# Whole fp32 operands in two products of each second projection's last piece, and a subtraction moved from GpSimd to VectorE

## The chip, the cores and the metric

The kernel runs on one core of a Trainium2 chip. Its engines are TensorE (PE in the profile; its weight loads are listed as PEld), VectorE (DVE), ScalarE (ACT), GpSimd (POOL) and SyncE (SP), which issues most DMAs. Each engine works through its own line of instructions in order and waits on semaphores of the others. The metric is the time of one execution on the device in microseconds; lower is better.

## The reference

A decoder trunk of two layers over 1024 positions with 1024 features, all in float32. Each layer is a token mixer and a gated feed-forward block (FFN), each behind an RMS norm with a scale and a shift that depend on the conditioning vector c.

```python
for layer in range(DEPTH):
    sh1, sc1, g1, sh2, sc2, g2 = jnp.split(c_act @ mod_w[layer] + mod_b[layer], 6, axis=-1)
    h = modulate(rmsnorm(x, norm_mix_g[layer]), sh1, sc1)
    y = dsa_mixer(h, ...) if layer == 0 else gmlp_mixer(h, ...)
    x = x + g1 * y
    h = modulate(rmsnorm(x, norm_ffn_g[layer]), sh2, sc2)
    x = x + g2 * ((silu(h @ w_gate) * (h @ w_up)) @ w_down)
return rmsnorm(x, final_g)

def gmlp_mixer(h, w_in, ln_g, ln_b, w_s, b_s, w_out):
    z = gelu(h @ w_in)
    u, v = z[..., :2048], layernorm(z[..., 2048:], ln_g, ln_b)
    v = v.reshape(B, 8, 128, 8, 256)                       # chunks of 128 positions, 8 groups
    mixed = einsum('gts,bcsge->bctge', w_s * tril, v) + b_s.T[:, :, None]
    return (u * mixed.reshape(B, T, 2048)) @ w_out
```

Layer 0 has the attention mixer, layer 1 the gMLP mixer.

## The kernel before

Activations stand transposed: features on the 128 partitions, positions along the free dimension, in two halves `ch` of 512 positions. Products that have to be precise are made from a value's high part (its cast to fp32r, by ScalarE) and its low part (the value less the high part, by VectorE or GpSimd); `mm3` (L177 to L181) adds three fp32r matmuls, high x high, high x low and low x high, in a PSUM bank.

There are four second projections, all made by `out_win` (L1009): the attention's output (one piece, n = 4), the first FFN's (pieces of 4, 4 and 3), the gMLP's (4 and 4) and the last FFN's (4, 4 and 3). A piece covers 2n blocks of 128 of the contracted features. Inside a piece the 2x2 blocks of weights (`wraw`, pages A and B) and of activations (`graw`, pages 1 and 2) are multiplied in Winograd's way, in seven products j in the order 1, 2, 6, 7, 4, 5, 3. Each product has 4 x n matmul groups. Before a product, `mv_prep` and `w_prep` make its sums from the raw pages and split them into high and low parts: `gm` (activations, n tiles, one page each) and `wst` (weights, 4 tiles). The cast is at L1057, the subtraction at L1058. Where the table `whole(pi)` names a product, the raw or summed fp32 values go to TensorE as they are, by L1164 instead of `mm3`:

```python
def whole(pi):
    if len(pieces) == 1:
        return RAW_1
    return RAW_F if pi == 0 else RAW_L if pi == len(pieces) - 1 else ()
```

Before, this holds for product 2 of a first piece where there are several pieces. After each group, `residual` (L952, VectorE) adds the PSUM bank times a gate to the residual stream `x`; the next product of the same four banks waits for it.

In the last piece, the norm of the next block begins between products: after product 4 the first half of `x` is complete, and `moving(ch=0)` makes its squares (`sqp`, ScalarE and VectorE), their sum over features on TensorE (`st`), the root, and a broadcast (`rb`, TensorE); `LOCK` puts part of product 5 behind `st` and part behind `rb`. Then VectorE makes `xr`, ScalarE `hq`, and they are split into `mv` for the next layer. Products 5 and 3 complete the second half, and `moving(ch=1)` follows.

The gMLP mixer loops over 8 groups g. A group makes seven products (3, 5, 4, 2, 1, 6, 7), each of four `mm3`, sums them on VectorE in pages `gu` and `uv`, and multiplies the four results with the mixed gate values `y` (`gate_fin`, L1537). The sum after product 7 is L1558; the first sums after products 3 and 2 are L1507. The gate values come from `mix_v`, one group ahead, twice for each group:

```python
ACT.copy(vh_, zg)
VL_ENG.tensor_sub(vl_, zg, f(vh_))
```

These are `vnh` (L1457) and `vnl` (L1458) of 128x1024; the mixing matmuls L1525 and L1526 read them. `VL_ENG` is GpSimd.

The order of each engine's line is written by a planner that simulates the program with estimated durations; `issue_after` adds single constraints. Tiles come from pools: 37 pages of 128x1024 fp32 (`pg`), 8 `wst` slots (`wsp`), 4 + 4 PSUM banks.

Of the kernel before, what the change touches and what calls it, by code (L numbers as in the profile page):

```python
# [102 lines left out]
PF_F = {3: 12, 2: 12, 7: 12, 6: 8, 5: 2}  # L103
PF_G = {4: 4, 2: 4, 7: 4, 1: 4, 3: 2, 6: 12}
VN_DVE = 1
RAW_F, RAW_1, RAW_L = (2,), (), ()
FF0 = (0,) * 6 + (4,) * 9 + (3,) * 4 + (0,) * 3
FF1 = (0,) * 8 + (1,) * 8 + (0,) * 6

# [4 lines left out]
def trunk(ctx, tc, xT, c, modT, vec, kgb, w_idx, w_q, w_a, wuk, wuv, wo, wg, wu, wd,  # L114
          bwu, bwv, bwo, bws, bbs, outT):
    nc = tc.nc
    PE, DVE, ACT, POOL, SP = nc.tensor, nc.vector, nc.scalar, nc.gpsimd, nc.sync
# [27 lines left out]
    def f(ap):  # L145
        return ap.bitcast(F32)
# [45 lines left out]
    SUM_ENG = {1: POOL, 2: POOL, 5: DVE, 6: POOL, 7: POOL}  # L192
    LO_ENG = {1: DVE, 2: DVE, 3: DVE, 4: POOL, 5: DVE, 6: DVE, 7: POOL}
    UA_ENG = POOL
    VL_ENG = POOL
    ident = cst.tile([P, P], F32, name="ident")
    make_identity(nc, ident)
    identr = cst.tile([P, P], F32R, name="identr")
# [1141 lines left out]
    def gmlp(x, B, pieces):  # L1340
# [104 lines left out]
        def mix_v(g, i):  # L1445
# [11 lines left out]
            ACT.copy(vh_, zg)  # L1457
            VL_ENG.tensor_sub(vl_, zg, f(vh_))  # L1458
            return vh_, vl_
# [222 lines left out]
```

## Time and profile before

| | |
|---|---|
| runs of the kernel before | 2596.45, 2601.79, 2601.98 us; median 2601.79 |
| the profiled execution | 2602.36 us, span 2600.7 us |
| mean granted clock of TensorE | 0.959 |
| busy, VectorE / ScalarE / GpSimd | 2133.6 / 1208.5 / 1344.0 us |

The span runs from the first to the last instruction of the program; the 1.7 us beside it are start and end. Times in rows are microseconds from the start of the span. In the rows, "out<-in" are the program's names, and what follows "idle before" is the time that the engine stood still just before the instruction, with what ended it.

### The profile page before, as it was taken

What the parts mean: (1) busy time and instruction counts of PE and PEld (TensorE: products, weight loads), DVE (VectorE), ACT (ScalarE), POOL (GpSimd) and SP (SyncE); (2) the same over time, 40 slices, a digit from 0 to 9 for tenths busy, and PEclk for the clock granted to TensorE, in tenths of its full rate; (3) what the DMA queues carried; (4) which work ended last, traced back from release to release, by engine and by line L of the source; (5) the groups of instructions that cost most, each with busy time, mean ns of one, the idle gap of its engine ahead of it and who ended that gap; (6) DMA issues with size and microseconds to landing.
All of it is one profiled execution on the core that took longest, in us unless ns stands there. A gap on an engine that the chain in (4) does not pass through costs nothing. (4 is left out here: it accounts for less than half of the span.)

```text
span 2600.7 us, 31048 instructions
## 1 busy us (share of the span) xinstructions
PE 2397.1 (92%) x10254; PEld 1877.9 (72%) x10254; DVE 2133.6 (82%) x3433; ACT 1208.5 (46%) x2223; POOL 1344.0 (52%) x962
## 2 busy tenths in 40 slices
PE   6979889988899999989988999988999999999996
PEld 4544577876688888768766877767767888886785
DVE  6497988898988888799878688899889666568986
ACT  5377775655533333343464454424464333333334
POOL 2021143465755556665556455566467444455663
PEclk7999899999999999999998999999999999999998
DMA  6002265645135544632123244363132223254021
GB/s 255 33 9 74 107 212 177 231 134 163 60 133 186 193 164 154 251 130 97 37 78 122 81 142 131 108 259 130 50 113 98 105 98 111 76 213 162 14 98 65
DMA packets 133919, 328.58 MB, mean 126 GB/s; under 512 B 14080, under 2 KB 30720, under 8 KB 133760
## 3 DMA queue, kind: packets, MB, share of 16 engines
q1 hardware_dynamic: 130432, 318.22, 34.7%
q0 software_dynamic: 3328, 8.39, 1.1%
q8 instruction: 81, 1.33, 0.2%
q14 instruction: 78, 0.64, 0.1%
HBM read 253.16 MB, written 73.40 MB: 126 GB/s over the span
## 5 line engine op out<-in xcount | busy, mean ns | idle before, releaser
L1239 PE MATMUL p<-mv,wst 128*128 128x512 f32 x1232 | 484.8, 394 | 9.2 <-DVE mv L967 9.2
L1240 PE MATMUL p<-mv,wst 128*128 128x512 f32 x1232 | 484.3, 393 | 7.2 <-DVE wst L1218 7.2
L1238 PE MATMUL p<-mv,wst 128*128 128x512 f32 x1232 | 483.1, 394 | 2.4 <-ACT wst L1217 0.9
L1216 POOL TENSOR_TENSOR wsum<-wgu 128x512 f32<-128x512 f32 x208 | 300.4, 1447 | 303.2 <-DVE wst L1218 198.4
L179 PE MATMUL d_ps<-gm,wst 128*128 128x512 f32 x904 | 366.2, 406 | 50.5 <-DVE x L952 44.6
L181 PE MATMUL d_ps<-gm,wst 128*128 128x512 f32 x904 | 359.0, 397 | 2.0 <-DVE wst L1058 2.0
L180 PE MATMUL d_ps<-gm,wst 128*128 128x512 f32 x904 | 359.3, 397 | 0.2 <-DVE gm L1058 0.2
L1239 PEld LDWEIGHTS p<-mv,wst 128*128 128x128 f32 x1232 | 233.7, 190 | 63.1 <-DVE mv L967 13.8
L1240 PEld LDWEIGHTS p<-mv,wst 128*128 128x128 f32 x1232 | 234.0, 190 | 57.8 <-DVE wst L1218 9.4
L1238 PEld LDWEIGHTS p<-mv,wst 128*128 128x128 f32 x1232 | 233.9, 190 | 54.8 <-issue 2.5
L1217 ACT CAST wst<-wsum 128x512 fp32r<-128x512 f32 x260 | 161.3, 621 | 216.9 <-POOL wsum L1216 97.1
L179 PEld LDWEIGHTS d_ps<-gm,wst 128*128 128x128 f32 x904 | 174.1, 193 | 98.9 <-ACT wst L1057 32.6
L1218 DVE TENSOR_TENSOR wst<-wsum,wst 128x512 fp32r<-128x512 f32 x208 | 200.6, 966 | 44.4 <-ACT wst L1217 43.4
L952 DVE SCALAR_TENSOR_TENSOR x<-d_ps,modv,x 128x512 f32<-128x512 f32 x252 | 185.0, 740 | 30.7 <-PE d_ps L181 30.7
L181 PEld LDWEIGHTS d_ps<-gm,wst 128*128 128x128 f32 x904 | 174.1, 193 | 40.7 <-DVE wst L1058 3.2
L180 PEld LDWEIGHTS d_ps<-gm,wst 128*128 128x128 f32 x904 | 174.6, 193 | 38.9 <-issue 1.7
L1058 POOL TENSOR_TENSOR gm<-graw,gm 128x512 fp32r<-128x512 f32 x102 | 158.8, 1566 | 81.9 <-ACT gm L1057 67.4
L1057 ACT CAST wst<-wraw 128x512 fp32r<-128x512 f32 (+1 forms) x204 | 117.3, 593 | 160.1 <-PE d_ps L181 137.2
L1057 ACT CAST gm<-graw 128x512 fp32r<-128x512 f32 x192 | 113.1, 618 | 102.2 <-DVE wst L1058 34.2
L1058 DVE TENSOR_TENSOR wst<-wraw,wst 128x512 fp32r<-128x512 f32 (+1 forms) x153 | 133.8, 878 | 13.2 <-ACT wst L1057 13.2
L1058 POOL TENSOR_TENSOR wst<-wraw,wst 128x512 fp32r<-128x512 f32 (+1 forms) x51 | 72.9, 1430 | 126.7 <-ACT wst L1057 126.7
L1217 ACT CAST wst<-wgu 128x512 fp32r<-128x512 f32 x104 | 64.3, 619 | 144.0 <-PE p L1240 70.8
(380 smaller groups left out, 5576.9 us busy)
## 6 DMA issues: line engine op xcount, KB each, us to landing
md<-modT SPq DMA_DIRECT2D x96, 512.0 KB, 5.3
wgu<-wg SPq DMA_DIRECT2D x56, 512.0 KB, 3.5
wgu<-wu SPq DMA_DIRECT2D x56, 512.0 KB, 4.4
g_d<-uv SPq DMA_DIRECT2D x88, 256.0 KB, 2.0
graw<-g_d SPq DMA_DIRECT2D x44, 512.0 KB, 7.6
wraw<-wd SPq DMA_DIRECT2D x64, 256.0 KB, 6.4
x_d<-x SPq DMA_DIRECT2D x48, 256.0 KB, 2.1
x<-x_d SPq DMA_DIRECT2D x24, 512.0 KB, 7.1
```

Source lines behind the costliest of these rows:

```text
L179: PE.matmul(ps, sh, mh, start=first, stop=False, skip_group_check=run)
L180: PE.matmul(ps, sh, ml, start=False, stop=False, skip_group_check=run)
L181: PE.matmul(ps, sl, mh, start=False, stop=last, skip_group_check=run)
L952: DVE.scalar_tensor_tensor(xk[:, cs], ps, gate, (xk[:, cs] if src is None else src), op0=ALU.mult, op1=ALU.add)
L1057: ACT.copy(t[:, 0, :n], s)
L1058: e.tensor_sub(t[:, 1, :n], s, f(t[:, 0, :n]))
L1216: SUM_ENG[j].tensor_tensor(s, o[0], o[1], op=o[2])
L1217: ACT.copy(t[:, 0], s)
L1218: LO_ENG[j].tensor_sub(t[:, 1], s, f(t[:, 0]))
L1238: PE.matmul(ps, sh, mh, start=k == 0, stop=False)
L1239: PE.matmul(ps, sh, ml, start=False, stop=False)
L1240: PE.matmul(ps, sl, mh, start=False, stop=k == 3)
```

## The change

Products 5 and 3 of the last piece of each second projection (the only piece of the attention's output) take their operands whole in fp32. `VL_ENG` becomes VectorE.

```diff
-RAW_F, RAW_1, RAW_L = (2,), (), ()
+RAW_F, RAW_1, RAW_L = (2,), (5, 3), (5, 3)
@@
-    VL_ENG = POOL
+    VL_ENG = DVE
```

## Rows read from the trace of the kernel before

**Rows 1.** The page, part 1: busy time, share of the span, instructions.

```profile
PE 2397.1 (92%) x10254; PEld 1877.9 (72%) x10254; DVE 2133.6 (82%) x3433; ACT 1208.5 (46%) x2223; POOL 1344.0 (52%) x962
```

**Rows 2.** Stretches: length, busy by engine (instructions), granted clock, DMA share, GB/s.

```profile
577.00:625.00 48.00, 40.41 (x161) 31.23 (x160) 42.71 (x73) 22.22 (x39) 20.78 (x14) 0.93 0.40 134
...
2537.00:2566.00 29.00, 22.58 (x88) 18.00 (x89) 23.25 (x33) 13.29 (x25) 7.67 (x6) 0.88 0.00 1
```

**Rows 3.** TensorE's waits, 575 to 645 us: us in total, times, longest.

```profile
PE d_ps L179 <- DVE x L952: 5.5, 4, 2.0
PE st L287 <- DVE sqp L284: 2.1, 1, 2.1
```

**Rows 4.** TensorE's waits, 1270 to 1340 us.

```profile
PE d_ps L179 <- ACT gm L1057: 4.6, 1, 4.6
PE z_ps L179 <- DVE xr L972: 2.5, 1, 2.5
...
PE d_ps L179 <- DVE x L952: 0.9, 1, 0.9
```

**Rows 5.** TensorE's waits, 1845 to 1912 us.

```profile
PE d_ps L179 <- DVE x L952: 4.0, 3, 1.7
```

**Rows 6.** TensorE's waits, 2535 us to the end.

```profile
PE d_ps L179 <- DVE x L952: 6.6, 2, 5.6
```

**Rows 7.** Timeline of VectorE from 2538 us: start, length, line, tiles, count.

```profile
2538.46 1.67 DVE L1058 TENSOR_TENSOR gm<-graw,gm 128x512 fp32r<-128x512 f32 x1
2540.06 1.62 DVE L1058 TENSOR_TENSOR wst<-wraw,wst 128x384 fp32r<-128x384 f32 x1
2541.60 0.74 DVE L952 SCALAR_TENSOR_TENSOR x<-d_ps,modv,x 128x512 f32<-128x512 f32 x1
```

**Rows 8.** TensorE's waits in the group loop, 1519 to 1714 us.

```profile
PE p L179 <- DVE uv L1558: 9.3, 4, 2.4
PE p L179 <- DVE uv L1507: 2.4, 2, 2.0
```

**Rows 9.** Timeline of VectorE in the group loop, from 1605 us.

```profile
1605.57 5.41 DVE L1537 TENSOR_TENSOR gu<-gu,y 128x512 f32<-128x512 f32 x2
1610.90 0.68 DVE L1558 TENSOR_TENSOR uv<-uv,p 128x512 f32<-128x512 f32 x1
```

**Rows 10.** Instructions of L1458: shortest/median/longest ns, first and last start.

```profile
L1458 POOLq EVENT_SEMAPHORE  x22: 17/43/4869, 1520.2 to 1687.3; - x22
L1458 POOL TENSOR_TENSOR vnl<-zg,vnh x16: 2390/2638/2946, 1521.4 to 1691.8; 128x1024 fp32r<-128x1024 f32 x16
```

**Rows 11.** Groups of VectorE, 1519 to 1714 us: busy, mean ns, idle before.

```profile
L1537 DVE TENSOR_TENSOR gu<-gu,y 128x512 f32<-128x512 f32 x14 | 32.4, 2338 | 0.0
...
L1545 DVE TENSOR_TENSOR uv<-uv,p 128x512 f32<-128x512 f32 x8 | 5.4, 676 | 0.0
```

**Rows 12.** A stretch of the group loop, columns as in the second group.

```profile
1600.00:1630.00 30.00, 27.38 (x127) 22.42 (x126) 24.62 (x42) 14.20 (x27) 16.12 (x11) 0.94 0.32 110
```

**Rows 13.** Timeline of TensorE: product 2 of the gMLP's first piece.

```profile
1734.12 13.89 PE L1164 MATMUL d_ps<-graw,wraw 128*128 128x512 f32 x32
```

**Rows 14.** A stretch of the first FFN, tile d_ps: length, PE, PEld, DVE, clock.

```profile
1182.40:1193.30 10.90, 10.90 (x49) 9.01 (x48) 2.87 (x4) 1.00 0.00 0
```

**Rows 15.** Groups by form, 575 to 630 us: the splits' subtractions on VectorE.

```profile
L1058 DVE TENSOR_TENSOR gm<-graw,gm 128x512 fp32r<-128x512 f32 x8 | 8.7, 1086 | 0.0
L1058 DVE TENSOR_TENSOR wst<-wraw,wst 128x512 fp32r<-128x512 f32 x11 | 8.2, 741 | 0.0
```

**Rows 16.** Timeline of TensorE: last matmul of the attention's output.

```profile
637.10 0.39 PE L181 MATMUL d_ps<-gm,wst 128*128 128x512 f32 x1
```

**Rows 17.** Timeline of VectorE: last addition of the attention's output.

```profile
642.19 0.74 DVE L952 SCALAR_TENSOR_TENSOR x<-d_ps,modv,x 128x512 f32<-128x512 f32 x1
```

**Rows 18.** Timeline of VectorE: a two-input operation on 128x1024.

```profile
598.77 1.21 DVE L246 SCALAR_TENSOR_TENSOR md<-md,cact 128x1024 f32<-128x1024 f32 x1
```

**Rows 19.** Timeline of GpSimd: an addition in the group loop.

```profile
1612.26 1.29 POOL L1216 TENSOR_TENSOR wsum<-wgu 128x512 f32<-128x512 f32 x1 [1.83 <-DVE wst L1218]
```

## The prediction

> **What bounds the kernel now.** I read the page's busy times first: no engine fills the span, TensorE comes nearest with 92% and VectorE follows with 82% [rows 1]. A share over the whole span decides nothing here, so I looked at the stretches that the change touches: the four ends of a second projection (attention output at 577 to 637 us, first FFN at 1274 to 1316, gMLP at 1849 to 1900, last FFN at 2537 to 2581) and the group loop of the gMLP mixer (1519 to 1714).
>
> In the ends TensorE is not full. At the attention output it works 40.4 of 48 us and VectorE 42.7; at the last FFN 22.6 of 29 with a granted clock of 0.88 [rows 2]. The view of TensorE's waits names who ends its idle time: a residual addition of VectorE, L952, which has to empty a PSUM bank before the next product may use it: 5.5, 4.0 and 6.6 us at the attention output, gMLP and last FFN [rows 3, 5, 6]; at the first FFN 4.6 us are booked to a cast of ScalarE [rows 4], but L952 ends at the same moment there, so I treat it alike. In VectorE's timeline the additions stand in line behind splits of later products: at the last FFN a 1.67 us `gm` split and a 1.62 us `wst` split stand ahead of the addition at 2541.60 [rows 7]. So these ends are bound by VectorE up to the fifth product, then by TensorE.
>
> In the group loop TensorE is the bound, but four times it waits for L1558, 9.3 us together [rows 8]. The timeline shows why: L1558 at 1610.90 waits behind two gate multiplications L1537 that take 5.41 us together [rows 9], each about as long as one of the `vnl` subtractions that GpSimd runs at that time, 2390 to 2946 ns [rows 10]. L1537 into `gu` takes 2338 ns on average in the loop, while an addition with one PSUM operand takes 676 [rows 11]. The granted clock of that stretch is 0.94 [rows 12]; the two stretches of 30 us after it show the same 0.94.
>
> **First edit, removed and added: products 5 and 3 from whole fp32.** It reaches all four projections (`RAW_1` the attention output, `RAW_L` the other three). With n = 4 there are 16 products of a 128x128 by a 128x512 block for each j, with n = 3 twelve, so 32 + 24 + 32 + 24 = 112 in all. Product 2 of a first piece already runs so: 16 products show as 32 matmuls in 13.89 us [rows 13]. The split form takes 48 matmuls in 10.9 us, 0.227 apart (the 49th was still running at the start of that stretch) [rows 14], some 11.04 with the end of the last one. The difference is 2.85 us for 16 products, 0.178 each: 5.7 us at the attention output and gMLP, 4.3 at the two FFNs, 20.0 together.
>
> Removed are the splits of these products: for n = 4 and both products 8 casts and 8 subtractions each for `gm` and `wst`; VectorE loses 4 `gm` (1086 ns) and 6 `wst` (741 ns), 8.8 us [rows 15], GpSimd the other 4 `gm` and 2 `wst`. At the FFNs VectorE loses 2 `gm` and 6 narrower `wst`. No DMA is added; the raw pages stay in use until their products are done, but the eight `gm` pages are not needed.
>
> What it is worth is read end by end, up to the start of the next layer's second statistics.
> Attention output: I take 3.5 us back of the 5.5 before product 5, since two or three of the `gm` splits between the additions go and the modulation dot products stay; of the 5.7 us, 0.7 vanish in the 2.1 us that TensorE waits for the first statistics [rows 3]. TensorE ends 5.7 - 0.7 - 3.5 = 1.5 us later. But after its last product VectorE is behind: its last addition starts at 642.19, 4.7 us after TensorE's last matmul ends at 637.49 [rows 16, 17], and its line starts 3.5 us earlier. I take -2.
> gMLP: both waits for L952 over 1 us go (3 of 4.0 us); VectorE is as far behind afterwards as at the attention output. I take -2.5.
> First FFN: about 1 us of the 4.6 goes; 0.5 of 4.3 is hidden by the 0.9 us wait. TensorE ends 2.8 us later, but it then waits 2.5 us for VectorE's `xr` [rows 4], which comes from statistics that only the first two or three of the eight slower blocks precede. I take +1.
> Last FFN: of the 5.6 us wait 1.67 go with the `gm` split and 1.0 with the `wst` split, which runs without GpSimd beside it in 0.6 (2.7 together); the clock of 0.88 over 29 us means 0.24 of that at the lower level of 1.2 GHz, some 3.5 us lost, and a shorter wait gives back 2 of them, by rows of the gMLP's end, where waits of up to 1.7 us [rows 5] leave no such trace. Price 4.3 - 0.5 = 3.8. I take -1.
> Sum of the first edit: -2 - 2.5 + 1 - 1 = -4.5 us. Its bounds: with no relief at all +17.6 (20.0 less the 0.7 + 0.5 + 0.7 + 0.5 hidden in the waits for statistics); with every wait for L952 gone and all price hidden at the three inner ends, 4.3 - 5.5 - 4.6 - 4.0 - 6.6 = -16.4.
>
> **Second edit, moved: 16 subtractions of 128x1024 from GpSimd to VectorE.** GpSimd's cost 2638 ns each, 42 us, go [rows 10]. VectorE has no such row; its nearest, a two-input operation on 128x1024, takes 1.21 us [rows 18]. So VectorE gains 19.4 us of work, and loses the lock on L1537, 14 x (2.34 - 0.68) = 23 us [rows 11]. In 30 us it has 5.4 free [rows 12], so its load is not the question, its order is. Today L1537 twice takes 5.41 us ahead of L1558. After, two multiplications at 0.68 and, if both come first, two subtractions at 1.21: 3.78 us. L1558 comes 1.6 us earlier if both stand ahead of it, and the wait of 2.3 us ends altogether if one stands behind. That is 6.6 to 9.3 us over the four waits. The clock of 0.94 over three stretches of 30 us means 3.6 us each at 1.2 GHz, 1.8 lost, 5.4 together; the wait left would be near 0.7. So 6.6 to 14.7. I take 8, near the low end, because another wait can become the last one: the loop already shows 2.0 us for L1507 [rows 8], which this edit does not touch.
>
> The Trainium skill, "SBUF — State Buffer", section "SBUF: two separate sides", states that VectorE and GpSimd hold a shared port pair as an exclusive lock for a whole instruction, also where a VectorE instruction has two SBUF inputs. The 2338 ns of L1537 agree, as does the undisturbed operation with a PSUM operand [rows 11]. The rule also speaks against the move: each moved subtraction has two SBUF inputs and can itself be held up by a GpSimd addition; by it the second edit would gain nothing, as in the third case below.
>
> **Sum.** The profiled execution took 2602.36 us (span 2600.7, 1.7 around it); the median of the three runs is 2601.79, 0.6 below. 2602.4 - 4.5 - 8 = 2589.9: I predict 2590 us, 0.5% faster. Less than 0.2%, about 5 us, can't be told from no change.
>
> **Rivals.**
> Forecast, 0.50: both gains come in part, 2580 to 2596.
> Slower, the price of whole fp32 decides, 0.18: TensorE is the end-setter behind product 5 and pays 17.6 us, the second edit gives its 8: 2602.4 + 17.6 - 8 = 2612. For it: behind the statistics TensorE has no wait left in product 5 or 3 of the attention output [rows 3]. Against it: VectorE's lag of 4.7 us. It decides once less than 10 us of the 20.7 us of L952-type waits (5.5 + 4.6 + 4.0 + 6.6) come back or are hidden.
> The wait moves to VectorE's own line, 0.15: a subtraction has to wait for its cast or its page, as GpSimd's did up to 4.87 us [rows 10], or for a GpSimd addition of 1.29 us [rows 19], and L1537 and L1558 queue behind it. With 1.29 more for each, the line ahead of L1558 is 1.35 + 2 x 2.5 = 6.35, 0.9 more than today, 3.8 us over four groups; the 8 us go: 2602.4 - 4.5 + 3.8 = 2602, no change.
> More than forecast, 0.17: the second edit gives 14.7 and the first 10: 2578.
> Against all: the order of each engine's line is written by a planner from estimated durations, and changed durations can reorder lines elsewhere; I widen by 2 us for it.
>
> **Numbers.** Range 2576 to 2612: it leaves out half of the best case and half of the slow one, some 0.17. The forecast's own range is 2580 to 2596. Faster than 2596.6: 0.50 + 0.17 = 0.67; slower than 2607: the slow rival, 0.18; between: 0.15.
>
> **What would show it.** First edit: 224 matmuls from `graw` and `wraw` more (96 become 320), each pair 0.87 us; the waits for L952 before product 7 and 5 shorter; VectorE's last addition no later than before measured from the end of product 4. Second edit: `vnl` on VectorE at 1.2 to 1.3 us (at 2.5, the lock rival holds); L1537 near 0.7; L1558's waits under 0.7; clock near 1.0 in the loop. I am wrong if TensorE runs dense through both last products and the next layer starts later by their whole price, or if VectorE idles ahead of `vnl`.

## The result and the profile after

The changed kernel takes 2569.92 us (median of four runs, 2564.94 to 2573.62) against 2601.89 (2596.45 to 2607.94) of the kernel before on the same chip: ratio 0.9871, 95% interval 0.9854 to 0.9888, 1.3% faster. The forecast was 2590 with a range of 2576 to 2612: the direction was right, the gain is more than twice the forecast one, and the time lies below the range. The profiled execution took 2573.62 us, its span 2571.9, 28.7 less than that of before.

The page, part 1, of the changed kernel (busy time, share, instructions), to be read against [rows 1]:

```profile
PE 2399.3 (93%) x10142; PEld 1850.6 (72%) x10142; DVE 2099.6 (82%) x3413; ACT 1178.7 (46%) x2163; POOL 1270.4 (49%) x922
```

This line already holds the sum. TensorE has 112 matmuls fewer (336 became 224), as it should, and by the forecast's price these cost 20.0 us more; but its busy time grew by 2.2 us only. So its other work took 17.8 us less, at a higher granted clock (0.959 to 0.965 over the span). Its time without work, span less busy, fell from 203.6 to 172.6 us, by 31.0. Together: +20.0 - 17.8 - 31.0 = -28.8, the span's 28.7 within rounding.

TensorE's waits in the four ends of the changed kernel (total, times, longest), in the order of [rows 3 to 6]:

```profile
PE d_ps L179 <- DVE x L952: 2.5, 2, 2.0
PE st L287 <- DVE sqp L284: 0.9, 1, 0.9
...
PE d_ps L179 <- DVE x L952: 3.6, 1, 3.6
...
PE d_ps L179 <- DVE x L952: 1.0, 1, 1.0
...
PE st L287 <- DVE sqp L284: 4.8, 1, 4.8
PE d_ps L179 <- DVE x L952: 3.6, 1, 3.6
```

The waits for L952 fell from 5.5 to 2.5 at the attention output, from 4.0 to 1.0 at the gMLP and from 6.6 to 3.6 at the last FFN; at the first FFN one of 3.6 us stands where 4.6 were booked to L1057 [rows 4]. What is left stands before or inside product 7, ahead of the changed products; at the attention output the 2.0 us before product 7 stayed as they were, and the waits of product 4 went. The whole-fp32 matmuls, one group of the whole span (busy, mean ns), and one dense stretch in TensorE's timeline:

```profile
L1164 PE MATMUL d_ps<-graw,wraw 128*128 128x512 f32 x320 | 140.7, 593 | 0.0
```

```profile
618.36 13.90 PE L1164 MATMUL d_ps<-graw,wraw 128*128 128x512 f32 x32
```

32 matmuls for 16 products in 13.90 us, as in [rows 13]: the price came as forecast.

The group loop of the changed kernel: TensorE's waits, groups of VectorE (busy, mean ns), the instructions of L1458 and their semaphore waits (shortest/median/longest ns) and VectorE's timeline at one gate product.

```profile
PE mx_ps L1525 <- DVE y L1531: 4.0, 7, 1.2
PE rw_ps L1438 <- DVE y L1531: 2.8, 2, 1.6
PE p L179 <- ACT wst L1217: 1.7, 1, 1.7
```

```profile
L1458 DVE TENSOR_TENSOR vnl<-zg,vnh 128x1024 fp32r<-128x1024 f32 x16 | 21.2, 1323 | 0.0
L1537 DVE TENSOR_TENSOR uv<-uv,y 128x512 f32<-128x512 f32 x14 | 12.5, 918 | 0.0
L1537 DVE TENSOR_TENSOR gu<-gu,y 128x512 f32<-128x512 f32 x16 | 11.6, 738 | 0.0
```

```profile
L1458 DVE TENSOR_TENSOR vnl<-zg,vnh x16: 1207/1219/2207, 1514.8 to 1679.3; 128x1024 fp32r<-128x1024 f32 x16
L1458 DVEq EVENT_SEMAPHORE  x10: 21/21/1094, 1513.2 to 1672.9; - x10
```

```profile
1599.28 1.29 DVE L1537 TENSOR_TENSOR gu<-gu,y 128x512 f32<-128x512 f32 x2
1600.49 0.68 DVE L1558 TENSOR_TENSOR uv<-uv,p 128x512 f32<-128x512 f32 x1
1601.69 1.22 DVE L1458 TENSOR_TENSOR vnl<-zg,vnh 128x1024 fp32r<-128x1024 f32 x1
```

The two multiplications ahead of L1558 take 1.29 us where they took 5.41 [rows 9], the subtraction stands behind L1558, and the 9.3 us of waits for it [rows 8] are gone. The whole loop, from the first mixing matmul to the last L1558, in the view of stretches (columns as in [rows 2]), before and then after:

```profile
1519.70:1727.50 207.80, 188.06 (x889) 156.67 (x890) 178.91 (x299) 95.54 (x170) 122.07 (x77) 0.94 0.45 156
```

```profile
1513.30:1704.40 191.10, 180.77 (x893) 151.19 (x894) 177.60 (x314) 96.43 (x170) 82.80 (x61) 0.99 0.47 165
```

16.7 us shorter: 9.4 less without work, and 7.3 less busy time for the same matmuls, at a granted clock of 0.99 instead of 0.94.

Executions differ by some microseconds before the attention's output begins (the same matmul starts at 563.0 to 577.7 us over all kernels below), so parts of the span are compared by stretches in us, each between two instructions of the one profiled execution of a kernel:

```
attention  first matmul of product 6 of its output -> L1293 of the first FFN's first unit
FFN 1      L1293 of the first FFN's last unit -> first mixing matmul L1525
loop       first mixing matmul -> last L1558
gMLP       last L1558 -> L1293 of the last FFN's first unit
FFN 2      L1293 of the last FFN's last unit -> end
                    attention  FFN 1   loop   gMLP  FFN 2
before                148.5    427.0  207.7  250.3  248.1
changed               142.8    422.8  191.1  245.0  247.8
changed, once more    143.5    422.0  190.4  245.3  248.1
raw_only              143.6    423.2  207.6  246.5  247.5
vl_only               149.8    428.1  192.7  249.7  246.1
no_vl                 146.6    428.6  188.1  250.6  247.8
vl_dummy              149.9    428.2  212.7  252.7  245.8
vl_pool_quarters      146.5    428.0  205.5  251.9  247.9
quarters_ua           147.4    428.2  203.0  247.0  247.8
quarters_mixadd       149.8    429.0  201.5  250.3  245.9
before_mixadd         147.5    428.3  210.6  250.3  246.2
splits_kept           155.1    430.5  191.7  254.4  249.4
raw_attn              142.0    429.6  193.7  250.5  247.9
raw_gmlp              147.5    427.6  190.0  245.7  247.4
raw_ffn               147.0    428.3  193.4  250.2  247.4
raw_attn_gmlp         142.0    429.1  194.6  246.4  247.3
raw_three             141.9    424.1  192.8  248.6  246.2
vn0                   142.6    423.5  190.2  246.1  247.8
after_mixadd          142.7    423.4  185.7  245.1  247.2
mixadd_again          143.5    421.9  186.5  244.8  247.0
```

### The profile page after: what moved, and what is told of

It is laid out like the page before. It is cut to its first block, busy times and chain, and to the rows that moved or that the text cites. A ratio compares the mean times of both kernels' runs of the same rounds, so it can differ in the third digit from the quotient of the medians.

```text
span 2571.9 us, 30703 instructions
## 1 busy us (share of the span) xinstructions
PE 2399.3 (93%) x10142; PEld 1850.6 (72%) x10142; DVE 2099.6 (82%) x3413; ACT 1178.7 (46%) x2163; POOL 1270.4 (49%) x922
## 5 line engine op out<-in xcount | busy, mean ns | idle before, releaser
L179 PE MATMUL d_ps<-gm,wst 128*128 128x512 f32 x792 | 317.8, 402 | 38.6 <-DVE x L952 38.0
L181 PE MATMUL d_ps<-gm,wst 128*128 128x512 f32 x792 | 313.4, 396 | 4.4 <-DVE wst L1058 4.4
L180 PE MATMUL d_ps<-gm,wst 128*128 128x512 f32 x792 | 313.6, 396 | 0.0
L1217 ACT CAST wst<-wsum 128x512 fp32r<-128x512 f32 x260 | 161.3, 621 | 202.8 <-PE p L1240 83.5
L952 DVE SCALAR_TENSOR_TENSOR x<-d_ps,modv,x 128x512 f32<-128x512 f32 x252 | 185.3, 742 | 40.1 <-PE d_ps L181 33.4
L179 PEld LDWEIGHTS d_ps<-gm,wst 128*128 128x128 f32 x792 | 152.4, 193 | 79.8 <-ACT wst L1057 25.3
L181 PEld LDWEIGHTS d_ps<-gm,wst 128*128 128x128 f32 x792 | 151.8, 192 | 37.6 <-DVE wst L1058 5.2
L180 PEld LDWEIGHTS d_ps<-gm,wst 128*128 128x128 f32 x792 | 152.1, 192 | 32.4 <-issue 0.5
L1058 POOL TENSOR_TENSOR gm<-graw,gm 128x512 fp32r<-128x512 f32 x86 | 132.2, 1545 | 74.7 <-ACT gm L1057 67.5
L1057 ACT CAST wst<-wraw 128x512 fp32r<-128x512 f32 (+1 forms) x172 | 99.4, 598 | 124.1 <-PE d_ps L181 104.5
L1164 PE MATMUL d_ps<-graw,wraw 128*128 128x512 f32 x320 | 140.7, 593 | 0.0
L1057 ACT CAST gm<-graw 128x512 fp32r<-128x512 f32 x164 | 96.7, 618 | 91.5 <-DVE wst L1058 30.7
L1217 ACT CAST wst<-wgu 128x512 fp32r<-128x512 f32 x104 | 64.4, 619 | 151.9 <-PE p L1240 76.4
L1218 POOL TENSOR_TENSOR wst<-wgu,wst 128x512 fp32r<-128x512 f32 x52 | 75.1, 1445 | 110.0 <-ACT wst L1217 110.0
```

Of the source, the lines that this page charges most:

```text
L179: PE.matmul(ps, sh, mh, start=first, stop=False, skip_group_check=run)
L180: PE.matmul(ps, sh, ml, start=False, stop=False, skip_group_check=run)
L181: PE.matmul(ps, sl, mh, start=False, stop=last, skip_group_check=run)
L952: DVE.scalar_tensor_tensor(xk[:, cs], ps, gate, (xk[:, cs] if src is None else src), op0=ALU.mult, op1=ALU.add)
L1057: ACT.copy(t[:, 0, :n], s)
L1164: PE.matmul(p, w[m][k], mv[k], start=first, stop=end, skip_group_check=j != 2)
```

## The experiments

Each ratio below is to the kernel before, run on the same chip.

**The two edits apart.** raw_only is the changed kernel with `VL_ENG = POOL`.

> The changed kernel with vnl back on GpSimd: the first edit alone. The forecast gave it -4.5 us. Theory A, from the milestones of the changed kernel's trace: everything that was gained outside the group loop belongs to it, 28.7 - 17 = about -12 us (2590). Theory B, the forecast's size holds: -4 to -5 us (2597), and the group loop gains more than 20 us by the second edit or the two help each other. Theory C, the whole fp32 products cost more than they give: 2605 or more, all gain comes from the second edit.

Measured: 2588.79 us, ratio 0.9952 (0.9937 to 0.9966), 12.5 us. vl_only is the changed kernel with the tables of before:

```diff
-RAW_F, RAW_1, RAW_L = (2,), (5, 3), (5, 3)
+RAW_F, RAW_1, RAW_L = (2,), (), ()
```

> The kernel before with vnl made by VectorE: the second edit alone. The forecast gave it -8 us, with bounds of -6.6 to -14.7 from the waits for L1558 and the lowered clock. Theory A, from the milestones of the changed kernel: -17 us in the group loop (about 2585), and the loop alone shows it. Theory B, the loop's gain is partly due to the first edit (it enters the loop with other work pending): -8 to -12 us, and raw_only and vl_only together fall short of 32 us. In the trace L1537 near 0.72 us, vnl near 1.2 to 1.3 us, no wait for L1558 over 0.7 us.

Measured: 2584.29 us, ratio 0.9933 (0.9918 to 0.9948), 17.4 us. Theory A holds for both. The edits act in different stretches: raw_only leaves the loop at 207.6 us, vl_only leaves the ends where they were. Their sum, 29.9 us, lies in the interval of the changed kernel (29 to 38 us).

**Second edit: an upper bound.** In no_vl nobody makes the low part; the mixing reads a page of zeros in its place:

```diff
-            vh_, vl_ = page("vnh", F32R), page("vnl", F32R)
+            vh_, vl_ = page("vnh", F32R), vz
...
-            VL_ENG.tensor_sub(vl_, zg, f(vh_))
```

> The kernel before with the subtraction vnl left out: the low part of the normalised gate value is read from one page of zeros, so the low part is missing from the output. Upper bound of the second edit: no engine makes vnl. If vl_only's 19 us of work on VectorE is hidden, no_vl and vl_only agree within 3 us (about 2585). If VectorE's share costs something, no_vl is 5 us or more below vl_only. If the forecast's bound of 14.7 us for waits and clock holds, no_vl is not under 2587; a lower time shows that more than the waits for L1558 and the half clock went away.

Measured: 2585.29 us, ratio 0.9942 (0.9922 to 0.9961), no different from vl_only. The loop alone is 4.6 us shorter than vl_only's in these two profiles: that much at most is what VectorE's own 21 us of subtractions cost there, since no_vl also needs no page for `vnl`.

**Second edit: GpSimd busy for nothing.** vl_dummy is vl_only with the same subtraction made again by GpSimd:

```diff
             VL_ENG.tensor_sub(vl_, zg, f(vh_))
+            POOL.tensor_sub(vd, zg, f(vh_))
```

> vl_only, and GpSimd makes the same subtraction again into a page that nobody reads. GpSimd holds up VectorE as before, but nothing waits for its result. Lock theory: L1537 is again near 2.3 us where the two meet, vnl on VectorE is held up too, and most of the gain is lost: 2597 or more (above the kernel before, if VectorE's own 16 subtractions suffer). Lateness theory (what cost time was that the mixing or the next GpSimd work had to wait for GpSimd's result): within 4 us of vl_only, 2584 to 2588.

Measured: 2608.33 us, ratio 1.0018 (1.0004 to 1.0032); the loop has 212.7 us, 20.0 more than vl_only's. VectorE's groups in its loop (line 1539 is the gate multiplication here), and a wait of TensorE's:

```profile
L1458 DVE TENSOR_TENSOR vnl<-zg,vnh 128x1024 fp32r<-128x1024 f32 x16 | 27.3, 1709 | 0.0
L1539 DVE TENSOR_TENSOR gu<-gu,y 128x512 f32<-128x512 f32 x16 | 19.1, 1202 | 0.0
L1539 DVE TENSOR_TENSOR uv<-uv,y 128x512 f32<-128x512 f32 x14 | 14.8, 1060 | 0.0
```

```profile
PE p L179 <- DVE uv L1509: 8.3, 7, 3.7
```

The whole gain of the move is lost though nobody needs the result: what cost time before was not that the mixing waited for `vnl`, but that GpSimd was at work on it. VectorE's two-input instructions are longer beside it (its subtractions 1709 ns against 1308 in vl_only, L1539 into `gu` 1202 against 789), but that multiplication does not come back to the 2.3 us that the lock theory named. The run can't separate this hold-up from GpSimd's own lateness for its other work (the wait for L1509 is for a subtraction that overwrites what GpSimd's addition reads), and its scratch page takes one of 37.

**Second edit: short pieces.** vl_pool_quarters is the kernel before with

```diff
-            VL_ENG.tensor_sub(vl_, zg, f(vh_))
+            for c in range(0, 1024, 256):
+                VL_ENG.tensor_sub(vl_[:, c:c + 256], zg[:, c:c + 256], f(vh_[:, c:c + 256]))
```

> The kernel before with each vnl subtraction of 128x1024 on GpSimd made as four of 128x256: the same work for GpSimd, in pieces of about 0.65 us. Lock theory (the long GpSimd instruction holds up VectorE's two-input instructions for its whole length): L1537 falls from 2338 ns on average to 1.3 us or less, the waits for L1558 lose more than half, and the time falls by at least half of what vl_only gives (8 us or more). Load theory (GpSimd's 42 us of work and its lateness are what costs): L1537 becomes shorter but the time stays within 3 us of the kernel before. Contention theory (VectorE runs slower beside any GpSimd work, in proportion to the overlap): L1537 stays near 2.3 us and the time does not change.

Measured: 2601.97 us, ratio 0.9999 (0.9988 to 1.001). The groups of the loop of before, then those of its own (L1538 is the gate multiplication, L1459 the piece) and the longest wait of TensorE:

```profile
L1537 DVE TENSOR_TENSOR gu<-gu,y 128x512 f32<-128x512 f32 x16 | 33.8, 2130 | 0.0
L1537 DVE TENSOR_TENSOR uv<-uv,y 128x512 f32<-128x512 f32 x14 | 10.3, 761 | 0.0
...
L1458 POOL TENSOR_TENSOR vnl<-zg,vnh 128x1024 fp32r<-128x1024 f32 x16 | 41.7, 2627 | 1.2 <-DMA wgu<-bwu 1.2
```

```profile
L1538 DVE TENSOR_TENSOR uv<-uv,y 128x512 f32<-128x512 f32 x14 | 16.9, 1236 | 0.0
L1538 DVE TENSOR_TENSOR gu<-gu,y 128x512 f32<-128x512 f32 x16 | 16.2, 1032 | 0.0
...
L1459 POOL TENSOR_TENSOR vnl<-zg,vnh 128x256 fp32r<-128x256 f32 x64 | 57.2, 927 | 0.6 <-DMA wgu<-bwu 0.6
```

```profile
PE p L179 <- DVE uv L1508: 8.3, 5, 2.5
```

The multiplication into `gu` fell from 2130 to 1032 ns (its mean over all 16; the 2338 of [rows 11] are for 14 of them) and the waits for the sum behind product 7 are gone, as the lock theory says; its time did not follow. The other multiplication rose from 761 to 1236, GpSimd needs 57.2 us instead of 41.7, and a wait of the same size appeared behind product 2, where a subtraction on VectorE must let GpSimd's addition read first. All three theories have a part of this and none its sum.

quarters_ua was meant to move that addition to VectorE. Its edit, `UA_ENG = DVE`, reaches the FFNs' 44 additions and not the mixer's, so it doesn't test what was expected of it:

> vl_pool_quarters, with the addition uA = v + u behind product 2 made by VectorE instead of GpSimd. In vl_pool_quarters the waits for L1558 were gone, but four waits of 1 to 2.5 us for a subtraction that overwrites u (8.3 us in all) had come, which has to let GpSimd's addition read u first. Theory A (two costs in series: the lock, and behind it GpSimd's lateness for that addition): with both gone TensorE's idle time in the loop falls from 22 to about 12 us, and the time to 2585 to 2592. Theory B (VectorE's line itself is late, whoever holds it up): the wait only moves to the next addition, and the time stays within 3 us of 2602.

Measured: 2600.21 us, ratio 0.9978 (0.9961 to 0.9995), the waits for L1508 still 8.0 us. The mixer's addition is a line of its own:

```diff
-            POOL.tensor_add(uA, v, u)
+            DVE.tensor_add(uA, v, u)
```

quarters_mixadd has it on top of the short pieces, before_mixadd on the kernel before.

> vl_pool_quarters (2602 us) with the mixer's addition uA = v + u, L1505, made by VectorE. Theory A, two costs in series (VectorE held up, and behind it GpSimd late for this addition): the four waits of 8 us for the subtraction that overwrites u go, idle time of TensorE in the loop falls from 22 to some 13 us, and the time to 2588 to 2594. Theory B, VectorE itself is late at that place, because each piece on GpSimd makes it slower: those waits stay within 2 us of 8, and the time within 4 us of 2602.

> The kernel before, vnl whole on GpSimd, with the mixer's addition L1505 made by VectorE. If the hold-up of L1537 by the long subtractions is what costs the loop its time, L1537 into gu stays near 2.3 us, the waits for L1558 stay near 9 us, and the time stays within 4 us of 2602. If GpSimd's lateness for L1505 is the cost, most of vl_only's 17 us come back: under 2592.

Measured: quarters_mixadd 2600.96 us, ratio 0.9972 (0.9956 to 0.9988), loop 201.5; before_mixadd 2607.51 us, ratio 1.0003 (0.9986 to 1.0021). TensorE's wait in quarters_mixadd, then the wait and the multiplication in before_mixadd's loop:

```profile
PE p L179 <- DVE uv L1508: 3.5, 3, 1.8
```

```profile
PE p L179 <- DVE uv L1558: 9.4, 5, 1.9
```

```profile
L1537 DVE TENSOR_TENSOR gu<-gu,y 128x512 f32<-128x512 f32 x16 | 33.7, 2128 | 0.0
```

GpSimd's late addition alone is not the cost: without it the long subtractions hold L1537 and L1558 up as before. With the long hold-up gone as well, the loop gains 6.2 us, less than theory A wanted (13 us of idle time; 17.2 are left). GpSimd works on `vnl` for 55 us there, and L1538 takes 1008 and 1264 ns beside it; that this is the reason was not tested further. Of the kernels tried, only those that take the work off GpSimd gain 15 us or more of the loop.

**First edit: the price without the relief.** splits_kept is the changed kernel with the unused high and low parts still made:

```diff
-                else:
+                if j not in whole(pi) or pi or len(pieces) == 1:
                     t = pg.tile([P, 2, CW], F32R, name="gm", tag="pg")
-                    r.append(split(t, s, CW, eng(GL_P, i)))
+                    q = split(t, s, CW, eng(GL_P, i))
+                    if j not in whole(pi):
+                        r.append(q)
```

and likewise for `wst`.

> The changed kernel, products 5 and 3 whole in fp32, but their high and low parts are still made on ScalarE, VectorE and GpSimd and go unused: the price of whole fp32 without its relief. If TensorE sets the end (the slow rival of the forecast), the price shows nearly whole, up to +17.6 us beside vl_only: about 2600. If VectorE's line sets the ends (splits, additions and the next norm), most of the price hides behind it: within 5 us of vl_only, 2584 to 2589, and the time is 14 us or more above the changed kernel, which is then the worth of the splits alone.

Measured: 2601.77 us, ratio 0.9989 (0.9979 to 1.0), 17.5 us above vl_only by the medians and 14.6 by the ratios. Up to the next layer's second statistics it is 20.5 us behind vl_only at the four ends together, the whole price; in the phases behind them 4.7 us come back, though no split was taken off (the table of the next section has both). TensorE's waits at its attention output, 570 to 660 us:

```profile
PE st L287 <- DVE sqp L284: 7.6, 2, 3.9
PE d_ps L179 <- DVE x L952: 6.9, 5, 2.2
```

They are as long as in the kernel before or longer: neither engine alone binds these ends. They wait for each other in turn, so time added to TensorE is not swallowed by VectorE's lateness, and the splits alone are worth 31.9 us between splits_kept and the changed kernel by the medians, 30.7 by the ratios. They stand on ScalarE and GpSimd too, and the unused parts hold pages beside the raw ones; this run does not separate these from VectorE's share.

**First edit: end by end, with vnl on VectorE.** raw_attn has `RAW_1 = (5, 3)` alone; raw_gmlp, raw_ffn and raw_attn_gmlp choose by the number of pieces (`== 3` in raw_ffn; raw_gmlp and raw_ffn also have `RAW_1 = ()`):

```diff
-            return RAW_F if pi == 0 else RAW_L if pi == len(pieces) - 1 else ()
+            return RAW_F if pi == 0 else RAW_L if pi == len(pieces) - 1 and len(pieces) == 2 else ()
```

> vnl on VectorE, and whole fp32 only in the attention's output (32 products). Beside vl_only (2584 us, ratio 0.9933). The forecast: -2 us for this end. Theory A, from the milestones of raw_only: -4 at the first FFN's first unit, of which some 2 us are lost again inside the first FFN, so -2 us in all. Theory B, the end does not matter because a later phase waits for something else anyway: 0.

> vnl on VectorE, and whole fp32 only in the gMLP's output (32 products). The forecast: -2.5 us beside vl_only. Theory A, from the milestones of raw_only (shift -6.0 at the end of the group loop, -9.8 at the last FFN's first unit): -4 us. Theory B, the group loop left earlier by the second edit already gives the end other conditions: between 0 and -2.

> vnl on VectorE, and whole fp32 only in the two FFNs' ends (48 products). The forecast: +1 at the first and -1 at the last, together 0 beside vl_only. Theory A, from the milestones of raw_only (first FFN: shift -2.0 at its last unit, -5.1 at the end of z; last FFN -0.7): -4 to -5 us, nearly all in the z phase behind the first FFN, where VectorE and ScalarE reach the splits of mv earlier. Theory B, the z phase's gain was a matter of chance in those profiles or came from the attention's end: within 1.5 us of vl_only.

> The changed kernel without whole fp32 in the two FFNs' ends. If the FFNs' products give their 5 us only beside the others, this is some 5 us slower than the changed kernel: ratio near 0.989 (2575). If they give nothing (raw_ffn alone: 0.9939, against 0.9933 of vl_only), it equals the changed kernel, ratio 0.987, and the first FFN's milestones show the gain without its own products. The first FFN from its last unit to the mixer's first matmul: 428 us without the edit, 423 in the changed kernel.

Measured ratios, beside 0.9933 of vl_only: raw_attn 0.9913 (0.9888 to 0.9939), raw_gmlp 0.9906 (0.9886 to 0.9925), raw_ffn 0.9939 (0.9919 to 0.9959), raw_attn_gmlp 0.9891 (0.9867 to 0.9916; 2579.53 us). Singly these intervals overlap; the stretches are finer. The attention's is 142.0 to 143.6 us in every kernel with its two products whole and 146.5 to 149.9 in those without (splits_kept apart). The gMLP's is 244.8 to 246.5 against 249.7 to 252.7 (left out: raw_three with its third product, and quarters_ua, whose moved FFN additions reach into this stretch). FFN 2 shows nothing. FFN 1 is 421.9 to 423.5 with all ends changed, 427.0 to 429.6 without its own products, and 428.3 in raw_ffn: its gain of 5 us needs its own products and yet did not come when the others were left out. In raw_ffn's trace TensorE's waits for `mv`, `zu` and `xr` did fall, to 10.2 us (12.5 in the changed kernel), but part of this is lost again (all engines' waits, 1385 to 1412 us):

```profile
POOL wsum L1358 <- DMA wzr<-bwv: 4.6, 1, 4.6
...
PE z_ps L179 <- ACT wz L1360: 2.7, 1, 2.7
```

A weight of the gMLP's input product comes late, GpSimd's sum and ScalarE's cast behind it. TensorE's waits for `wz` are 4.1 us in its z phase; the changed kernel has none. Why the load is later there was not tried; the planner writes every line anew for each kernel.

**First edit: a third product.** raw_three has (4, 5, 3) in both tables.

> The changed kernel, with product 4 of each last piece in whole fp32 too: 56 more products at 0.178 us, a price of 10.0 us. Relief theory as it stands (VectorE's splits of every late product cost more than fp32 does): another 3 to 8 us faster than the changed kernel. Rival (behind product 7 TensorE is dense in the changed kernel, no wait for a residual addition over 0.5 us is left there): 5 to 10 us slower than the changed kernel, 2575 to 2580.

Measured: 2579.82 us, ratio 0.9901 (0.9872 to 0.993). The relief theory is refuted: no gain. The rival fits the difference to the changed kernel's ratio, 7.8 us, but the two intervals overlap, and the four ends together are only 2.4 us longer in the profiles (1060.8 for 1058.4). Most of the price of 10.0 us thus came back: at the attention output the waits for L952, 2.5 us in the changed kernel, are gone. Behind product 7 there was none left to give back.

**Versions that could be faster.** vn0 is the changed kernel with `VN_DVE = 0`:

> The changed kernel, with all four blocks of zg normalised by ScalarE (VN_DVE = 0) instead of one of four by VectorE: 16 operations of 0.46 us less on VectorE, which is now the busiest engine of the group loop beside TensorE (181 of 195 us). Theory A (VectorE's load makes the waits of 4.0 and 2.8 us that are left for y): 2 to 4 us faster than the changed kernel, as no_vl's loop was 3 to 4 us shorter. Theory B (the order is what holds, and ScalarE's cast of vnh comes later): no change, or 2 us slower.

Measured: 2573.3 us, ratio 0.9872 (0.9842 to 0.9902), no change: theory B. after_mixadd is the changed kernel with L1505 on VectorE:

> The changed kernel with the mixer's addition L1505 made by VectorE: a version that could beat it. GpSimd is then left with the weights' sums alone. If GpSimd's remaining two-input instructions still hold VectorE up in the loop (L1537 at 0.74 to 0.96 us instead of 0.68, vnl at 1.32 instead of 1.21), 2 to 4 us faster than the changed kernel. If VectorE's line (181 of 195 us) is the limit, 2 to 5 us slower.

Measured: 2567.78 us, ratio 0.9838 (0.9812 to 0.9864). Then both side by side:

> The changed kernel once more, as the measure for mixadd_again on the same chip: ratio to the kernel before 0.985 to 0.989.

> after_mixadd once more: the changed kernel with the mixer's addition L1505 on VectorE. If the 5.4 us that its loop gained in the profile (idle time of TensorE 6.8 us instead of 11.0) are real: 4 to 7 us below after_again, ratio 0.983 to 0.985. If they were the spread of runs: within 2 us of after_again.

Measured: the changed kernel 2568.30 us, ratio 0.9863 (0.9842 to 0.9884), this one 2563.74, ratio 0.9837 (0.9821 to 0.9853). Its four runs, 2561.04 to 2566.22, all lie under the four of the changed kernel, 2567.2 to 2574.36. Its loop as a stretch, and a group of VectorE in it (L1505 is the moved addition):

```profile
1509.40:1695.90 186.50, 180.06 (x901) 152.28 (x902) 179.68 (x320) 96.82 (x170) 71.44 (x54) 0.99 0.50 174
```

```profile
L1505 DVE TENSOR_TENSOR gu<-uv 128x512 f32<-128x512 f32 x7 | 5.5, 787 | 1.7 <-ACT uv L1502 1.7
```

The loop has 186.5 us, and 185.7 in the first profile, against 191.1 and 190.4. It beats both kernels, by 4.6 us the changed one: VectorE makes in 787 ns what GpSimd made in 1.3 to 1.5 us, and the subtraction behind it (L1507) no longer waits for GpSimd, as it did for 1.4 us in the changed kernel. On the kernel before the same edit was worth nothing (before_mixadd).

## Why the forecast had the direction and not the size

Two sizes failed. The first edit's relief was taken too small, and it was counted only up to a point behind which nearly as much again came. The second edit was taken at half its worth. The directions and the named waits were right.

**What bounds the kernel** was read rightly as far as the runs reach: the waits for L952 in the ends and those for L1558 in the loop went, and the time with them.

**The price**, 20.0 us for 112 products, is right: 13.90 us per 16 products, and splits_kept pays 14.6 to 17.5 us in the time where the slow rival put 17.6 into the sum. That rival was to decide if less than 10 us of the waits for L952 came back. Some 10 us did (20.7 became 10.7), and more came beside them.

**The relief of the first edit** is the first mis-sized term. The forecast added the ends up to the next layer's second statistics, -4.5 us, and put what lies behind them at nothing, without a reason. The table has the differences to the kernel before in us, from the starts of the stretches above to the first matmul of the second statistics (`st`), and from there to the end of the stretch:

```
                    up to the second statistics         behind them
                    attn.  FFN 1  gMLP  FFN 2    sum    attn.  FFN 1  gMLP  FFN 2    sum
forecast            -2.0   +1.0   -2.5  -1.0    -4.5     0      0      0     0        0
changed             -3.3   -0.8   -3.5  -0.7    -8.3    -2.4   -3.4   -1.8  +0.4    -7.3
changed, once more  -4.2   -1.3   -3.3  -0.5    -9.3    -0.8   -3.7   -1.6  +0.4    -5.6
raw_only            -3.9   -0.7   -1.5  -0.6    -6.7    -1.0   -3.1   -2.3   0.0    -6.3
vl_only             +1.4   +0.9   +0.5  -2.0    +0.8    -0.2   +0.2   -1.1   0.0    -1.1
splits_kept         +7.4   +6.6   +5.9  +1.4   +21.3    -0.8   -3.1   -1.8   0.0    -5.8
```

So two things were missed. Up to the statistics the relief is 29.6 us (splits_kept against the changed kernel) where the forecast had 17.6 + 4.5 = 22.1. Behind them another 5.6 to 7.3 us come. They come in splits_kept too, where every split is still made, so they do not need the relief of VectorE; why they come no run shows.

At the attention output the waits for L952 fell much as forecast (by 3.0 us of the 3.5). TensorE's part, from product 6 to its last matmul, in two stretches of before and then of after:

```profile
567.70:594.90 27.20, 23.82 (x98) 18.93 (x96) 27.20 (x39) 17.96 (x33) 15.57 (x10) 0.94 0.23 77
...
608.60:637.49 28.89, 26.78 (x113) 21.45 (x112) 24.08 (x36) 20.35 (x35) 17.71 (x13) 0.94 0.60 192
```

```profile
569.39:594.20 24.81, 22.33 (x98) 17.87 (x97) 24.78 (x40) 11.54 (x21) 8.95 (x6) 1.00 0.32 106
...
605.20:637.29 32.09, 31.20 (x83) 14.78 (x82) 27.43 (x38) 20.02 (x33) 18.88 (x14) 1.00 0.63 213
```

A granted clock of 0.94 over 27.2 and 28.9 us means that 0.12 of each ran at the lower of the two levels (1.2 GHz) and 0.06 was lost: 1.6 + 1.7 = 3.3 us, which the forecast did not count here and which are gone after. The first 1.6 us are not the edit's: the wait of 2.0 us before product 7 stands in both traces, and the same stretch shows 1.00 in eight of the ten kernels without these products whole, and 0.93 in vn0, which has them. The other 1.7 us are: TensorE stood still for 2.1 us for the statistics there [rows 3], 0.9 after, and the clock of this stretch is 0.89 to 0.94 in eight of the ten kernels without whole products and 1.00 in all with them (0.95 in splits_kept). So TensorE did not end 1.5 us later, as forecast, but 1.9 earlier (67.9 us for 69.8, with 13.7 and 11.0 us for product 4 in between). The other kernels bear this out: 67.7 to 71.3 us without whole products here, 65.7 to 67.9 with them, splits_kept apart. Behind its last product the next layer's first phase shortened by 3.8 us. That this is close to the 3.5 of the forecast is luck: the lag of VectorE that was to shrink stayed, its last addition starts 4.6 us after TensorE's last matmul, 4.7 before.

The gMLP: -5.3 in these two profiles instead of -2.5. TensorE ended 1.5 us later there; VectorE's lag fell from 5.8 to 2.1 us, and the phase behind shortened from 78.0 to 71.3 us. It is 70.8 to 71.5 us in every kernel with these products whole, splits_kept too, and 74.4 to 79.2 in the others. The first FFN: -4.2 instead of +1. Its term ended at the next statistics. In the z phase the waits of before for `mv`, `zu` and `xr` (1316 to 1520 us), and after, are:

```profile
PE z_ps L179 <- ACT mv L966: 6.9, 4, 4.0
PE z_ps L181 <- DVE mv L967: 5.8, 2, 4.6
PE z_ps L179 <- DVE zu L1404: 2.6, 1, 2.6
```

```profile
PE z_ps L179 <- DVE zu L1404: 4.8, 1, 4.8
PE z_ps L181 <- DVE mv L967: 3.9, 3, 2.4
PE z_ps L179 <- ACT mv L966: 3.8, 2, 3.5
```

With the 2.5 us for `xr` [rows 4], which are gone, 17.8 us became 12.5. The last FFN: -0.3 instead of -1. The clock over that end, which the forecast wanted to rise, stayed where it was: 0.93 over 45.7 us before and over 45.5 after.

**The second edit** is the other mis-sized term: 8 us were taken out of bounds of 6.6 to 14.7 (the lower one is 6.5 by its own numbers, 4 x 1.63), and vl_only gives 15.0 us in its loop, the upper end. Its loop as a stretch, then those of raw_only and of the changed kernel once more:

```profile
1519.80:1712.40 192.60, 182.83 (x894) 153.55 (x895) 180.66 (x313) 97.00 (x170) 80.41 (x61) 0.97 0.49 169
```

```profile
1513.90:1721.50 207.60, 187.82 (x901) 155.58 (x902) 179.71 (x299) 95.33 (x170) 122.41 (x77) 0.97 0.46 159
```

```profile
1507.10:1697.50 190.40, 180.78 (x884) 151.80 (x885) 178.14 (x314) 96.49 (x170) 81.81 (x61) 0.97 0.48 168
```

Against the loop of before that is 10.0 us less without work, the 9.3 us of waits for L1558 above all, and 5.2 us less busy time. That the 5.2 us are the lost clock (5.4 in the forecast) is not shown. raw_only has 0.97 where before has 0.94, with `vnl` on GpSimd in both, and its loop is as long and as busy (207.6 and 187.8 us); the changed kernel once more has 0.97 for 0.99, with the same 180.8 us of work. raw_only and vl_only have the same 0.97 and differ by 15.0 us. So in these kernels the engine that makes `vnl` sets the length of the loop and the mean clock does not; how much of the busy time is the clock's stays open. The reason given for the low end, that another wait would become the last one, did not hold: the 2.4 us for L1507 became 1.8 in vl_only and 0.4 in the changed kernel.

**The rivals.** The one called "more than forecast" (0.17, 2578 us) came nearest: the second edit gave its 14.7 us, the first 12.5 for its 10. The bounds of both edits together reach 2602.4 - 16.4 - 14.7 = 2571.3, so the range, which ended at 2576, was narrower than its own sum allowed. The rival that the wait moves into VectorE's own line is refuted: the subtractions take 1219 ns in the middle and 2207 at most, their wait for an input is at most 1.09 us, and L1558 no longer waits behind them. They are not free: ScalarE's cast of the next weights (L1217) waits for them seven times, 10.0 us in all, and TensorE once for such a cast (1.7 us). The Trainium skill's rule of the exclusive lock ("SBUF — State Buffer", section "SBUF: two separate sides") fits vl_dummy, where both engines subtract at once and VectorE's take 1709 ns; by that rule alone the move would have gained nothing, and the measurement decides against this reading of it. The instruction that held others up was GpSimd's 2.6 us one, and it is gone.

**Of the marks** named for it: each pair 0.87 to 0.88 us, 320 matmuls, `vnl` at 1.2, L1537 into `gu` at 0.74, no wait for L1558, clock 0.99 in the loop (0.97 once more): these came. The multiplication into `uv`, at 918 ns, is slower than the 761 before. Two marks did not come. The wait before product 7 of the attention output is as long as before (2.0 us). And VectorE's last addition, measured from the end of product 4, starts later at all four ends: 36.5 us for 33.4 at the attention output, 25.0 for 22.7 at the first FFN, 32.9 for 30.5 at the gMLP, 25.1 for 21.7 at the last FFN. What the attention output and the gMLP gained up to the statistics they gained ahead of that point (5.1 and 4.7 us).

## What to carry to other kernels

A wait of a microsecond or two between dense matmuls can cost more than itself where the granted clock falls behind it (1.7 us at the attention's statistics), and need not: behind the same wait of 2.0 us the clock fell in one of the two traces and not in the other. (1 - clock) times the stretch says what was lost, not what a change gives back; compare kernels that differ in the clock alone before counting on it. Do not end the sum at the first point where the engines meet: more than a third of what the first edit gained came behind it. Where two engines wait for each other in turn, count price and relief separately, and stop where no wait is left (the third product gained nothing). In this loop a long two-input instruction on GpSimd was paid for by VectorE, even when nobody needed its result; cutting it into pieces spread the cost, taking it away ended it.

## What was not expected of the hardware

Short pieces did not shorten the loop. Four subtractions of 128x256 on GpSimd took 927 ns each, 3.7 us for the 128x1024 that took 2.6 in one. VectorE's longest hold-ups fell (L1537 into `gu` from 2130 to 1032 ns), the other multiplication rose from 761 to 1236 ns; VectorE's busy time in the loop fell from 178.9 to 172.9 us, and the loop only from 207.7 to 205.5.

TensorE's busy time grew by only 2.2 us although 20 us of work were added to it. The higher clock can account for at most 16.6 of the 17.8 us that came back: 0.041 of 2600.7 us were lost before and 0.035 of 2571.9 after, waits included. The rest is open, and so is the clock's true share: two executions of the kernel before on one chip had 0.959 and 0.965 and took 2603.02 and 2604.34 us.
